# A planned diffusion layer in float32: the first small loads go to ScalarE's queue, single features' weights to another ring, and the planner gets other times for warm-ups and for the probabilities' trip

## The chip, the cores and the metric

The kernel runs on one core of one Trainium2 chip. What counts is the time of one execution on the device, in microseconds, as the median of several runs. TensorE (PE) multiplies matrices, VectorE (DVE) and ScalarE (ACT) work elementwise, GpSimd (POOL) does a little set-up work, and SyncE (SP) issues transfers, which 16 DMA engines carry out.

## What is computed

One layer of a diffusion transformer, on 256 latent tokens and 256 context tokens of width 2048, all in float32:

```python
sh1, sc1, g1, sh2, sc2, g2 = ada_mods(c, w_ada, b_ada)          # silu(c) @ w_ada + b_ada; six vectors of 2048
csh1, csc1, ...            = ada_mods(c_ctx, w_ada, b_ada)
qa, ka, va, qb, kb, vb     = mixer_qkv(x * (1 + sc1) + sh1, w_in, ..., rope)        # w_in: 2048 x 3072
qac, kac, vac, ..          = mixer_qkv(ctx * (1 + csc1) + csh1, w_in, ..., None)
heads = concat(window_sink_attention(qa, ka, va, kac, vac, sink), global_attention(qb, kb, vb, kbc, vbc))
x = layer_norm(ALPHA * x + g1 * (heads @ w_out))
x = layer_norm(ALPHA * x + g2 * swiglu(x * (1 + sc2) + sh2, w_gate, w_up, w_down))   # hidden 5632
```

There are 16 query heads of 128 in four groups (two windowed with a sink, two global), each group with its own key and value head. `w_ada` is 2048 x 12288, `w_out` 2048 x 2048.

## The kernel before, in words

**Arithmetic.** A float32 product runs as three products of rounded parts: every operand is split into `hi` (a cast on ACT) and `lo` (the rest, a subtraction on DVE), and `mm3` (L271 to L273) issues `hi x hi`, `lo x hi` and `hi x lo`, each 128x512 on PE. So each weight tile that is loaded (`raw`) costs ACT a cast (L495, L261) and DVE a subtraction (L498, L262) before PE can use it, and its buffer comes free when both are done.

**First stage.** The features of the model are taken in growing groups (1, 1, 2, 4 and 8 blocks of 128). For each group the columns of `sh1` and `sc1` are computed first: `flow_columns` loads pieces of `w_ada` and multiplies them by `cs`, the silu of the two condition vectors, on PE (L546); the sums are copied by ACT (L571), added up on PE (L576) and given their bias `bcol`. Then x and the context are transposed on PE (L633), modulated on ACT (L639), split, and multiplied by the group's rows of `w_in` (`flow_blocks`), whose sums are kept in SBUF between groups. Before the first product PE runs warm-ups (L1130), multiplications of the identity that keep its clock up; `WARM` of them are steps of the plan with the lowest rank.

**Attention.** Sixteen pairs of heads (`flow_attend`: four for each head group) go the same way: scores on PE (six products for two heads), the row maximum on DVE, the exponentials and their weighting on ACT, a transposition in 32x32 squares on DVE (L921), then the probabilities' trip through memory, which puts the squares in order: a *put* of four transfers from `hx` to the scratch `pd` (L927), and a *get* of one transfer from `pd` to `pT` (L932), both issued by SP; the get waits until the put has landed. Then PE multiplies `pT` by the values (L939), and the results feed the output products with `w_out`. Beside all this DVE sums the gate `g1` from `w_ada` (L381), whose loads SP issues too (L371).

**What sets the order.** All steps up to the first FFN products are given to a planner, `Flow`: a step has an engine, a time in ns, steps that it follows, and buffers that it takes and gives back. `forward` runs them through a list schedule, `backward` ranks them by their latest start, eight times in turn, and the best order is written out: each engine executes its steps strictly in that order. On SP a load counts its transfer time (`dma_ns`: 390 bytes per ns for long rows) as the time of its step, and 2000 ns more until others may use it. A pair (step, early) in `after` lets the next step start `early` ns before the usual time, or later where `early` is negative. In the trip the put counts 1800 ns on SP, the get may start 1500 ns (`SLOW`) after it and counts 1300, and the products with the values may start 2000 + 1500 ns after that. `begin` holds the time at which each engine can start.

**Buffers.** `raw` (4) and `araw` (2) are 8 KB for each partition and hold weights as loaded; `hl` (4) holds pairs of hi and lo; `b4` is a ring of 18 buffers of 4 KB that holds operands, keys, `hx`, `pT` and the like. A buffer of a pool whose name ends in `raw` comes back 1300 ns after its last user in the plan (`AGAIN`).

**Start.** SP issues five small loads first: the two condition vectors (`crow`, L311 and L312), the biases (`brow`, L314), and the first blocks of x and of the context (L608, L613), and then the first pieces of `w_ada` and `w_in` (L473). The single features' weights (groups 0 and 1) come in four loads of 1, 2, 2 and 1 blocks of 512 columns, into `raw` or `araw`.

After the plan comes the FFN (L1344 on), in an order written by hand: gate and up products with u2 (`u2h`, `u2l`), then the down products with `hT`.

Of the kernel before, what the change touches and what calls it, by code (L numbers as in the profile page):

```python
# [22 lines left out]
P = 128  # L23
# [13 lines left out]
G4 = 4  # L37
# [8 lines left out]
T2K = 5  # L46
WARM = 56
SLACK = 2500
AHEAD = 14
# [5 lines left out]
SEED_G = 4  # L55
SLOW = 1500


class Buf:

    def __init__(self, *pools):
        self.pools, self.pool, self.left = pools, None, 0

# [5 lines left out]
class Flow:  # L69
# [26 lines left out]
    def forward(self):  # L96
# [11 lines left out]
        while len(order) < len(self.steps):  # L108
# [3 lines left out]
            for e in self.ENGINES:  # L112
# [4 lines left out]
                for item in sorted(ready[e]):  # L117
# [10 lines left out]
                    for b in s.give:  # L128
                        left[b] -= 1
                        if left[b] == 0:  # L130
                            lag = self.AGAIN if b.pool.endswith("raw") else self.OTHER[e]
                            heapq.heappush(back, (free[e] + lag, b.pool))
# [64 lines left out]
def dit_layer(ctx: ExitStack, tc: tile.TileContext, x, c, cx, c_ctx, w_ada, b_ada, w_in, q_norm_g,  # L197
# [112 lines left out]
    crow = pa.tile([2 * KD, P], F32, tag="crow", name="crow")  # L310
    nc.sync.dma_start(crow[0:KD, :], c.rearrange("o (k p) -> (o k) p", p=P))  # L311
    nc.sync.dma_start(crow[KD : 2 * KD, :], c_ctx.rearrange("(k p) -> k p", p=P))  # L312
    brow = pa.tile([6 * KD, P], F32, tag="brow", name="brow")
    nc.sync.dma_start(brow, b_ada.rearrange("o (n p) -> (o n) p", p=P))  # L314
    cps = wk_bank()
# [109 lines left out]
    def const_tables():  # L425
        nc.gpsimd.tensor_scalar_mul(nsink, sinkb, -1.0)
        for t in range(NT):
            for g, cg, sg in ((gq, cosQ, sinQ), (gk, cosK, sinK)):
# [18 lines left out]
    F = Flow({"raw": RAW_BUFS, "araw": ADA_BUFS, "hl": HL_BUFS, "acc": 4, "wk": 4, "b4": NB4, "t2k": T2K},  # L447
             {"SP": 2100.0, "PE": 3800.0, "ACT": 4300.0, "DVE": 4000.0, "POOL": 4000.0})
    pools = {"raw": wraw, "araw": araw}
    qacc = [[pa.tile([P, NB], F32, tag=f"q{gi}{t}", name="qacc") for t in range(NT)] for gi in range(4)]  # L450
# [17 lines left out]
    def flow_load(w, k0, nk, c0, width, where=("raw", "araw")):  # L468
        room = Buf(*where)

        def fn():
            room.t = pools[room.pool].tile([P, G4 * NB], F32, tag="raw", name="raw")[:, : nk * width]
            nc.sync.dma_start(  # L473
                room.t.rearrange("p (k n) -> p k n", k=nk),
                w[k0 * P : (k0 + nk) * P, c0 : c0 + width].rearrange("(k p) n -> p k n", p=P),
            )
# [124 lines left out]
    def flow_part(k0, n, at, each):  # L601
        ns = KD * n * P // (G4 * NB)
        ats = [at + each * 0.8 * (i + 0.5) / ns for i in range(ns)]
        copy, ready = flow_columns(k0 * P, n, shc[:, k0 : k0 + n, :], scc[:, k0 : k0 + n, :], ats, at + 0.8 * each)
        cx_room = Buf("b4")

        def load_x():
# [9 lines left out]
        ns = dma_ns(n * P * SEQ * 4, n * P * 4)  # L617
        loads = [F.add("SP", max(ns, 500), load_x), F.add("SP", max(ns, 500), load_cx, take=[cx_room])]
        for s in range(2):
# [3 lines left out]
            for j0 in range(0, n, 2):  # L623
# [24 lines left out]
                def rest(rooms=rooms, j0=j0, nj=nj, uf=uf):  # L648
                    nc.vector.tensor_tensor(rooms[1].t[:, j0 : j0 + nj, :], uf.t[:, :nj, :],
                                            rooms[0].t[:, j0 : j0 + nj, :].bitcast(F32), op=ALU.subtract)  # L650

                p = F.add("PE", 205 * nj, flip, [loads[s], copy if k0 else None], [ps], [cx_room] if s else [],
                          at=None if k0 else -1.0)
# [50 lines left out]
    def flow_blocks(g, bs, where=("raw", "araw")):  # L704

        k0, n = GROUPS[g]
        if n == 1:
            for i, (b0, m) in enumerate(((2, 1), (0, 2), (3, 2), (5, 1))):
                F.at = bs[0] + (bs[1] - bs[0]) * i / 4
                piece, = flow_weights(w_in, k0, 1, b0 * NB, m * NB, where)  # L710
                for j in range(m):
                    flow_block(g, b0 + j, [(piece, [j * NB])])
            return
# [149 lines left out]
    def flow_attend(gi, at, each):  # L863
# [5 lines left out]
        for p in range(4):  # L869
# [94 lines left out]
            for i in range(2):  # L964
                g.append(F.add("DVE", 615, lambda i=i, f=squares: f(i), [n[i], *g], [hx] if i == 0 else [], [probs[i]]))
            a = F.add("SP", 1800, put, g, give=[hx])
            g = [(F.add("SP", 1300, get, [(a, -SLOW)], [pT]), -SLOW)]
            v = F.add("PE", 1760, values, g, [o_ps], [pT, *kv_room[w]])
# [172 lines left out]
    for i in range(WARM):  # L1141
        warms.append(F.add("PE", 225, lambda i=i: warm_step(i), [warms[-1]], [wps] if i == 0 else [], [wps], at=1e6))

# [481 lines left out]
```

## Time and profile before

| | |
|---|---|
| runs | 1160.09, 1164.0 and 1165.95 us; median 1164.0 |
| span of the profiled execution | 1167.2 us, 3.2 above the median; what lies around the span is not listed |
| PE busy | 1130.9 us, 97% |
| weight loads of PE (PEld) | 912.2 us, 78% |
| DVE busy | 829.0 us, 71% |
| ACT busy | 546.9 us, 47% |
| moved by DMA | 321.28 MB, mean 275 GB/s |

PE busy counts a matmul until its modelled end, and matmuls overlap, so 100% busy is not yet PE at its peak; the weight loads beside it tell more: in stretches where one product follows on another they take some 0.19 us of each 0.23. A wait is told by the idle time before an instruction, with the engine or transfer that ended it. For SP the time of an instruction is that of issuing, not of moving data; DMA share and GB/s of a stretch tell what the engines moved. The mean of the DMA share can lie a little above 1.

### The profile page before, as it was taken

What the parts mean: (1) busy time and instruction counts of PE and PEld (TensorE: products, weight loads), DVE (VectorE), ACT (ScalarE), POOL (GpSimd) and SP (SyncE); (2) the same over time, 40 slices, a digit from 0 to 9 for tenths busy, and PEclk for the clock granted to TensorE, in tenths of its full rate; (3) what the DMA queues carried; (4) which work ended last, traced back from release to release, by engine and by line L of the source; (5) the groups of instructions that cost most, each with busy time, mean ns of one, the idle gap of its engine ahead of it and who ended that gap; (6) DMA issues with size and microseconds to landing.
All of it is one profiled execution on the core that took longest, in us unless ns stands there. A gap on an engine that the chain in (4) does not pass through costs nothing.

```text
span 1167.2 us, 14247 instructions
## 1 busy us (share of the span) xinstructions
PE 1130.9 (97%) x5347; PEld 912.2 (78%) x5347; DVE 829.0 (71%) x1053; ACT 546.9 (47%) x784; POOL 36.8 (3%) x82
## 2 busy tenths in 40 slices
PE   8999999999988989999999999999999999999995
PEld 8767678777866868888878888888888888888884
DVE  4754479899978978777757666676675778676556
ACT  3332454777755345444454444444444334343341
POOL 1000030111000000000000000000000000000000
PEclk9989999999999999999999999999999999999998
DMA  8999999777999859989967666767767988887641
GB/s 262 378 369 349 391 369 349 256 230 222 312 330 331 301 185 327 350 292 309 325 195 252 222 222 223 245 218 259 250 219 250 326 289 320 315 294 246 212 145 72
DMA packets 186271, 321.28 MB, mean 275 GB/s; under 512 B 8621, under 2 KB 51021, under 8 KB 183896
## 3 DMA queue, kind: packets, MB, share of 16 engines
q1 hardware_dynamic: 186200, 320.36, 79.5%
q8 instruction: 42, 0.69, 0.2%
q14 instruction: 29, 0.23, 0.1%
HBM read 304.07 MB, written 16.25 MB: 274 GB/s over the span
## 4 chain that ended last, share of the span: by engine, by line
PE 78%; DMA 9%; DVE 9%; issue 2%; ACT 1%; SPq 1%; DVEq 0%; ACTq 0%
PE acc L271 24%; PE acc L273 24%; PE acc L272 24%; DMA raw<-in_w_ada_dram 5%; PE wk L546 2%; DVE lo L498 2%; DMA pd<-hx 2%; PE wk L1130 1%; DVE g1b L381 1%; DMA pT<-pd 1%; SPq L927 1%; PE wk L939 1%; DVE hx L921 1%; DMA raw<-in_w_in_dram 1%; DVE adav L381 1%
## 5 line engine op out<-in xcount | busy, mean ns | idle before, releaser
L262 DVE TENSOR_TENSOR lo<-raw,hi 128x1024 fp32r<-128x1024 f32 x258 | 312.6, 1221 | 188.1 <-ACT hi L261 184.7
L261 ACT CAST hi<-raw 128x1024 fp32r<-128x1024 f32 x258 | 271.4, 1055 | 355.0 <-PE acc L273 310.4
L272 PE MATMUL acc<-lo,u2h 128*128 128x512 f32 x704 | 275.2, 391 | 2.3 <-DVE lo L262 2.3
L271 PE MATMUL acc<-hi,u2h 128*128 128x512 f32 x704 | 275.6, 391 | 1.2 <-ACT u2h L1448 1.2
L273 PE MATMUL acc<-hi,u2l 128*128 128x512 f32 x704 | 274.9, 391 | 0.0
L272 PEld LDWEIGHTS acc<-lo,u2h 128*128 128x128 f32 x704 | 132.8, 189 | 30.1 <-DVE lo L262 2.7
L271 PEld LDWEIGHTS acc<-hi,u2h 128*128 128x128 f32 x704 | 132.7, 189 | 28.9 <-ACT u2h L1448 1.4
L273 PEld LDWEIGHTS acc<-hi,u2l 128*128 128x128 f32 x704 | 132.8, 189 | 28.2 <-DVE u2l L1449 0.6
L495 ACT CAST hi<-raw 128x1024 fp32r<-128x1024 f32 (+1 forms) x86 | 87.8, 1032 | 120.7 <-DMA raw<-in_w_in_dram 60.3
L271 PE MATMUL acc<-hi,hTh 128*128 128x512 f32 x344 | 135.5, 394 | 0.0
L273 PE MATMUL acc<-hi,hTl 128*128 128x512 f32 x344 | 133.9, 389 | 0.0
L272 PE MATMUL acc<-lo,hTh 128*128 128x512 f32 x344 | 133.9, 389 | 0.0
L381 DVE SCALAR_TENSOR_TENSOR adav<-raw,cs,adav 128x512 f32<-128x512 f32 (+1 forms) x128 | 121.2, 947 | 14.0 <-DMA raw<-in_w_ada_dram 12.3
L498 DVE TENSOR_TENSOR lo<-raw,hi 128x1024 fp32r<-128x1024 f32 (+1 forms) x86 | 101.7, 1196 | 28.9 <-ACT hi L495 28.9
L271 PE MATMUL acc<-hi,uh 128*128 128x512 f32 x256 | 103.1, 403 | 0.2 <-ACT hi L495 0.2
L272 PE MATMUL acc<-lo,uh 128*128 128x512 f32 x256 | 100.5, 393 | 0.8 <-DVE lo L498 0.8
L273 PE MATMUL acc<-hi,ul 128*128 128x512 f32 x256 | 100.4, 392 | 0.0
L272 PEld LDWEIGHTS acc<-lo,hTh 128*128 128x128 f32 x344 | 64.6, 188 | 14.3 <-issue 1.0
L271 PEld LDWEIGHTS acc<-hi,hTh 128*128 128x128 f32 x344 | 64.6, 188 | 14.1 <-issue 0.7
L273 PEld LDWEIGHTS acc<-hi,hTl 128*128 128x128 f32 x344 | 64.6, 188 | 13.5
L271 PEld LDWEIGHTS acc<-hi,uh 128*128 128x128 f32 x256 | 48.5, 189 | 17.3 <-issue 5.8
L272 PEld LDWEIGHTS acc<-lo,uh 128*128 128x128 f32 x256 | 48.4, 189 | 10.6 <-DVE lo L498 1.2
(205 smaller groups left out, 1155.1 us busy)
## 6 DMA issues: line engine op xcount, KB each, us to landing
raw<-in_w_ada_dram SPq DMA_DIRECT2D x72, 1024.0 KB, 7.4
raw<-in_w_gate_dram SPq DMA_DIRECT2D x44, 1024.0 KB, 5.2
raw<-in_w_up_dram SPq DMA_DIRECT2D x44, 1024.0 KB, 5.5
raw<-in_w_down_dram SPq DMA_DIRECT2D x44, 1024.0 KB, 5.0
raw<-in_w_ada_dram SPq DMA_DIRECT2D x48, 512.0 KB, 5.1
raw<-in_w_in_dram SPq DMA_DIRECT2D x18, 1024.0 KB, 6.8
raw<-in_w_out_dram SPq DMA_DIRECT2D x16, 1024.0 KB, 5.7
pd<-hx SPq DMA_DIRECT2D x64, 128.0 KB, 5.7
```

The lines of the kernel that those rows point to most:

```text
L261: nc.scalar.copy(hi[:, :n], raw[:, s : s + n])
L262: nc.vector.tensor_tensor(lo[:, :n], raw[:, s : s + n], hi[:, :n].bitcast(F32), op=ALU.subtract)
L271: nc.tensor.matmul(ps, lhsT=xh, rhs=w[0], start=first, stop=False, skip_group_check=seeded)
L272: nc.tensor.matmul(ps, lhsT=xh, rhs=w[1], start=False, stop=False, skip_group_check=seeded)
L273: nc.tensor.matmul(ps, lhsT=xl, rhs=w[0], start=False, stop=last, skip_group_check=seeded)
L381: nc.vector.scalar_tensor_tensor(a[:, c : c + piece], raw[:, f : f + piece], cs[:, 4 * (g * (G4 * NB // w) + j) + 2, None], a[:, c : c + p ...
L495: nc.scalar.copy(hl.hi[:, :n], raw.t[:, s : s + n])
L498: nc.vector.tensor_tensor(hl.lo[:, :n], raw.t[:, s : s + n], hl.hi[:, :n].bitcast(F32), op=ALU.subtract)
L546: nc.tensor.matmul(bank.t[32 * j : 32 * j + 32, :width], lhsT=cs[:, 4 * k + 2 - 2 * i : 4 * k + 34 - 2 * i], rhs=raw.t[:, c * width : (c + ...
L921: nc.vector.transpose(hx.t[:, i, :].rearrange("p (r k q) -> p k r q", r=4, k=4), probs[i].t.rearrange("p (k r q) -> p k r q", r=4, k=4))
L927: nc.sync.dma_start(st["hd"][:, :, :, a, :].rearrange("r i h x -> i h r x"), hx.t[32 * a : 32 * a + 32].rearrange("i h (r x) -> i h r x", ...
L939: nc.tensor.matmul(o_ps.t[:, : 2 * P].rearrange("p (g q) -> p g q", q=32), lhsT=v, rhs=pv[:, k], start=k == 0, stop=k == 3)
```

## The change

1. The five small loads go from SP to ACT, ahead of ACT's first instruction; the first block of the context goes to the last 128 columns of `xt` for the time being (`first_cx`; x's own last columns are loaded there much later), and the planner no longer has load steps for the first block. SP's begin in the plan goes from 2100 to 900 ns. Three warm-ups stand ahead of the first transposition.
2. The single features' weights come in three loads of two blocks, and only into `b4`; a buffer counts as loaded (`AGAIN`) by the pools that it may use.
3. The first ten planned warm-ups count 430 ns, not 225.
4. The put counts 2700 ns, the get may start 3000 ns after it, and counts 1300 as before; the values' further wait stays at 1500, now `SLOW2`.

The core of the diff:

```diff
+EARLY_WARM = 3
+COLD = 10
-SLOW = 1500
+SLOW = 3000
+SLOW2 = 1500
+PUT_NS = 2700
+GET_NS = 1300
...
-        self.pools, self.pool, self.left = pools, None, 0
+        self.pools, self.pool, self.left, self.loaded = pools, None, 0, "raw" in pools[0]
...
-                            lag = self.AGAIN if b.pool.endswith("raw") else self.OTHER[e]
+                            lag = self.AGAIN if b.loaded else self.OTHER[e]
...
-    nc.sync.dma_start(crow[0:KD, :], c.rearrange("o (k p) -> (o k) p", p=P))
-    nc.sync.dma_start(crow[KD : 2 * KD, :], c_ctx.rearrange("(k p) -> k p", p=P))
+    nc.scalar.dma_start(crow[0:KD, :], c.rearrange("o (k p) -> (o k) p", p=P))
+    nc.scalar.dma_start(crow[KD : 2 * KD, :], c_ctx.rearrange("(k p) -> k p", p=P))
+    nc.scalar.dma_start(xt[:, :, :P], x[:, :P].rearrange("(t p) d -> p t d", p=P))
+    first_cx = xt[:, :, D - P :]
+    nc.scalar.dma_start(first_cx, cx[:, :P].rearrange("(t p) d -> p t d", p=P))
     brow = pa.tile([6 * KD, P], F32, tag="brow", name="brow")
-    nc.sync.dma_start(brow, b_ada.rearrange("o (n p) -> (o n) p", p=P))
+    nc.scalar.dma_start(brow, b_ada.rearrange("o (n p) -> (o n) p", p=P))
+    early = wk_bank()
+    for _ in range(EARLY_WARM):
+        nc.tensor.matmul(early[:, :P], lhsT=ident, rhs=ident, start=True, stop=True)
...
-             {"SP": 2100.0, "PE": 3800.0, "ACT": 4300.0, "DVE": 4000.0, "POOL": 4000.0})
-    pools = {"raw": wraw, "araw": araw}
+             {"SP": 900.0, "PE": 3800.0, "ACT": 4300.0, "DVE": 4000.0, "POOL": 4000.0})
+    pools = {"raw": wraw, "araw": araw, "b4": pa}
...
-            room.t = pools[room.pool].tile([P, G4 * NB], F32, tag="raw", name="raw")[:, : nk * width]
+            if room.pool == "b4":
+                room.t = b4([P, SUB * NB], F32, "raw4")[:, : nk * width]
+            else:
+                room.t = pools[room.pool].tile([P, G4 * NB], F32, tag="raw", name="raw")[:, : nk * width]
...
-        loads = [F.add("SP", max(ns, 500), load_x), F.add("SP", max(ns, 500), load_cx, take=[cx_room])]
+        loads = [F.add("SP", max(ns, 500), load_x), F.add("SP", max(ns, 500), load_cx, take=[cx_room])] if k0 else [None, None]
...
-            for i, (b0, m) in enumerate(((2, 1), (0, 2), (3, 2), (5, 1))):
-                F.at = bs[0] + (bs[1] - bs[0]) * i / 4
-                piece, = flow_weights(w_in, k0, 1, b0 * NB, m * NB, where)
+            for i, (b0, m) in enumerate(((2, 2), (0, 2), (4, 2))):
+                F.at = bs[0] + (bs[1] - bs[0]) * i / 3
+                piece, = flow_weights(w_in, k0, 1, b0 * NB, m * NB, ("b4",))
...
-            a = F.add("SP", 1800, put, g, give=[hx])
-            g = [(F.add("SP", 1300, get, [(a, -SLOW)], [pT]), -SLOW)]
+            a = F.add("SP", PUT_NS, put, g, give=[hx])
+            g = [(F.add("SP", GET_NS, get, [(a, -SLOW)], [pT]), -SLOW2)]
...
-        warms.append(F.add("PE", 225, lambda i=i: warm_step(i), [warms[-1]], [wps] if i == 0 else [], [wps], at=1e6))
+        warms.append(F.add("PE", 430 if i < COLD else 225, lambda i=i: warm_step(i), [warms[-1]], [wps] if i == 0 else [], [wps], at=1e6))
```

Since the planner works with other times, the order of every engine changes up to the FFN. Two places on SP matter most.

The first is the start of SP's program. In the kernel before, the rows up to the second pair of `w_ada` pieces are these (128x16x128 is a piece of 1 MB of one block's columns):

```order
L311 DMA crow<-in_c_dram 16x128
L312 DMA crow<-in_c_ctx_dram 16x128
L314 DMA brow<-in_b_ada_dram 96x128
L608 DMA xt<-in_x_dram 128x2x128
L613 DMA cxt<-in_ctx_dram 128x2x128
L473 DMA raw<-in_w_ada_dram 128x16x128 x2
L473 DMA raw<-in_w_in_dram 128x512
L473 DMA raw<-in_w_in_dram 128x1024 x2
```

In the changed kernel SP's program starts so (L487 is the same line as L473 before; raw_185, raw_190 and raw_211 lie in `b4`; 128x8x256 is a piece for a group of two blocks):

```order
L487 DMA raw<-in_w_ada_dram 128x16x128 x2
L487 DMA raw_185<-in_w_in_dram 128x1024
L487 DMA raw_190<-in_w_in_dram 128x1024
L487 DMA raw_211<-in_w_in_dram 128x1024
L487 DMA raw<-in_w_ada_dram 128x16x128 x2
L487 DMA raw<-in_w_ada_dram 128x8x256 x2
```

The five small loads have left the head of the queue, and two more pairs of `w_ada` pieces stand right behind the first weights. On ACT the five loads stand ahead of the table load and of everything else, in this order: the two condition vectors, x, the context, the biases. On PE 21 warm-ups stand ahead of the first products with `w_ada` before and 9 after, and 46 and 40 ahead of the first product with `w_in`.

The second place is the probabilities' trips, as SP has them from the fourth put on, in the kernel before (pd<-hx are the four transfers of a put, pT<-pd is a get, and the numbers tell which get belongs to which put):

```order
L927 DMA pd_2352<-hx_2306 64x4x128 x4
L932 DMA pT_2396<-pd_2352 128x1024
L473 DMA raw_2454<-in_w_out_dram 128x4x512
L927 DMA pd_2479<-hx_2458 64x4x128 x4
L932 DMA pT_2527<-pd_2479 128x1024
L473 DMA raw_2545<-in_w_out_dram 128x4x512
L927 DMA pd_2590<-hx_2540 64x4x128 x4
L932 DMA pT_2639<-pd_2590 128x1024
```

And in the changed kernel, from the fourth put on (L942 is the put, L947 the get, L382 a load for the gate):

```order
L942 DMA pd_2259<-hx_2215 64x4x128 x4
L947 DMA pT_2301<-pd_2171 128x1024
L382 DMA raw_2309<-in_w_ada_dram 128x2048
L947 DMA pT_2345<-pd_2259 128x1024
L487 DMA raw_2359<-in_w_out_dram 128x4x512
L942 DMA pd_2419<-hx_2398 64x4x128 x4
L487 DMA raw_2461<-in_w_out_dram 128x4x512
L947 DMA pT_2508<-pd_2419 128x1024
L942 DMA pd_2535<-hx_2499 64x4x128 x4
L487 DMA raw_2580<-in_w_out_dram 128x4x512
L947 DMA pT_2633<-pd_2535 128x1024
```

Before, each get stands right behind its own put; now a load or another pair's transfer stands between. Over the whole attention that is so: 6 of the 16 gets stood right behind their puts before and 1 after, and between put and get of the 11th, 12th, 13th and 16th pair there now stand 2 to 2.5 MB of other transfers, where 1 MB stood before. PE's order was moved with it: between the last score product of a pair and its first product with the values there stand on average 78.8 products of 128x512 before (60 to 108) and 94.9 after (60 to 132); the mean of the first eight pairs goes from 81.0 to 99.8, that of the last eight from 76.5 to 90.0, and three pairs lose (the fifth and the fifteenth 12 each, the tenth 6).

More of the change, by code (lines that the diff above doesn't have):

```diff
@@ L605, in flow_part @@
         cx_room = Buf("b4")
+        cx_room.t = first_cx
         def load_x():
@@ L650, in rest @@
                                             rooms[0].t[:, j0 : j0 + nj, :].bitcast(F32), op=ALU.subtract)
-                p = F.add("PE", 205 * nj, flip, [loads[s], copy if k0 else None], [ps], [cx_room] if s else [],
+                p = F.add("PE", 205 * nj, flip, [loads[s], copy if k0 else None], [ps], [cx_room] if s and k0 else [],
                           at=None if k0 else -1.0)
```

## The prediction

> **What bounds the kernel now.** I read the page first, then the busy time by stages, then the chain of waits and SP's rows for the two places that the change touches. The page says that PE is what the span is made of, and that the DMA engines are nearly full through the first third:
>
> ```profile
> span 1167.2 us, 14247 instructions
> ...
> PE 1130.9 (97%) x5347; PEld 912.2 (78%) x5347; DVE 829.0 (71%) x1053; ACT 546.9 (47%) x784; POOL 36.8 (3%) x82
> ...
> DMA  8999999777999859989967666767767988887641
> ```
>
> By stages (stretch, its length, busy time and instructions of PE, weight loads, DVE, ACT and POOL, granted clock, DMA share, GB/s):
>
> ```profile
> 0.00:20.00 20.00, 16.87 (x166) 16.05 (x167) 5.73 (x9) 6.14 (x12) 3.48 (x9) 1.00 0.74 224
> 20.00:150.00 130.00, 127.39 (x773) 88.61 (x772) 70.99 (x102) 44.91 (x69) 0.00 (x0) 0.97 1.01 372
> 150.00:240.00 90.00, 90.00 (x421) 73.56 (x422) 80.98 (x114) 57.52 (x108) 15.69 (x28) 1.00 0.86 316
> 240.00:300.00 60.00, 56.60 (x265) 45.08 (x265) 55.35 (x114) 42.69 (x112) 7.99 (x26) 1.00 0.74 225
> 300.00:400.00 100.00, 91.69 (x397) 73.46 (x396) 83.11 (x110) 56.61 (x93) 0.56 (x3) 0.98 1.00 340
> 400.00:480.00 80.00, 76.33 (x360) 60.55 (x359) 64.26 (x94) 38.89 (x58) 3.19 (x6) 0.98 0.75 262
> 480.00:1100.00 620.00, 617.69 (x2736) 510.25 (x2735) 429.65 (x460) 279.12 (x309) 5.85 (x10) 1.00 0.77 264
> ```
>
> Five stages with three limits. From 20 to 150 the DMA share is 1.01: the weights' arrival sets the pace, and PE's weight loads fill only 68% of the time against 82% afterwards. From 150 to 240 PE has no idle time. In the attention, 240 to 400, PE is idle for 160 - 56.60 - 91.69 = 11.7 us, with DMA slack in the first 60 us (share 0.74) and none in the last 100 (1.00). From 480 on PE is full and the change touches nothing. So whatever the first 400 us win or lose reaches the end whole.
>
> **The start.** The chain of waits runs through PE's warm-ups (start, length, what; two records each):
>
> ```profile
> 3.83 1.76 PE wk L1130 x8
> ...
> 6.88 4.61 PE wk L1130 x32
> ...
> 12.49 2.65 PE wk L1130 x22
> ...
> 17.14 2.56 PE wk L1130 x22
> 19.70 0.23 PE acc L271
> ```
>
> A warm-up takes 1.76 / 4 = 0.44 us at first and 2.65 / 11 = 0.24 later, where the plan has 225 ns: by the plan PE was free sooner than it was. But from 20 us on DMA is the limit, so what counts in the start is when the transfers begin and whether they go on. SP's rows (start, length of issuing):
>
> ```profile
> 0.74 0.39 SPq L311 DMA_DIRECT2D crow<-in_c_dram  x1
> ...
> 3.09 0.47 SPq L473 DMA_DIRECT2D raw<-in_w_ada_dram  x1
> 3.60 1.65 SPq L473 DMA_DIRECT2D raw<-in_w_ada_dram  x1
> 5.29 3.65 SPq L473 DMA_DIRECT2D raw<-in_w_in_dram  x1
> ...
> 15.76 0.43 SPq L473 DMA_DIRECT2D raw<-in_w_ada_dram  x1
> ```
>
> The first large load is issued at 3.09, behind five small ones; and the next pair of `w_ada` pieces at 15.76, when a buffer is free. Between, the DMA engines run dry (same columns as above):
>
> ```profile
> 13.00:14.00 1.00, 1.00 (x12) 1.00 (x11) 0.00 (x0) 0.45 (x1) 0.00 (x0) 1.00 0.54 209
> 14.00:15.00 1.00, 1.00 (x11) 0.95 (x9) 0.69 (x1) 0.16 (x1) 0.00 (x0) 1.00 0.03 12
> 15.00:16.00 1.00, 1.00 (x34) 0.81 (x32) 0.00 (x0) 0.00 (x0) 0.00 (x0) 1.00 0.25 16
> 16.00:17.00 1.00, 1.00 (x17) 0.92 (x9) 0.00 (x0) 0.78 (x2) 0.00 (x0) 1.00 0.66 127
> ```
>
> *Term 1.* The changed SP starts with the large loads: 3.09 - 0.74 = 2.35 us. With the single features' weights in `b4` the six 8 KB buffers are left to `w_ada`, and 4 MB of it and 1.5 MB of `w_in` can be issued before any buffer must come back: 15 us at the 372 GB/s of the next stage, which reaches over the hole: 0.46 + 0.97 + 0.75 + 0.34 = 2.5 us. The small loads still have to be moved, beside the large ones now:
>
> ```profile
> xt<-in_x_dram SPq DMA_DIRECT2D x2, 128.0 KB
> cxt<-in_ctx_dram SPq DMA_DIRECT2D x2, 128.0 KB, 2.5
> brow<-in_b_ada_dram SPq DMA_DIRECT2D x1, 48.0 KB, 1.7
> ```
>
> One of each is 304 KB, 0.8 us at 372 GB/s. So 2.35 + 2.5 - 0.8 = 4.0 us of lead. Two later holes can go or grow with the new order:
>
> ```profile
> 85.00:90.00 5.00, 5.00 (x22) 4.22 (x21) 3.37 (x5) 4.06 (x9) 0.00 (x0) 0.76 0.56 172
> 100.00:105.00 5.00, 5.00 (x39) 1.90 (x38) 2.75 (x4) 0.00 (x0) 0.00 (x0) 1.00 0.74 251
> ```
>
> They lose 5 x 0.44 + 5 x 0.26 = 3.5 us. Bounds of the term: 0, if ACT's queue is slow (a rival below); 7.5, if these two holes close as well, which nothing says. The Trainium skill (DMA: Bandwidth & Descriptors, § Issuing engines are not separate DMA queues) says that DMAs of several issuers share the same engines, so that a second issuer saves only issuing time. By that alone the term would be 2.35; the hole is closed by buffers, which the page doesn't speak of.
>
> The rest of the start is free. What follows ACT's issues now, and when the first columns are multiplied:
>
> ```profile
> 1.05 1.28 ACT L319 ACT_TABLE_LOAD   x1 [1.05 <-DVE cs L318]
> 3.20 0.23 ACT L319 ACTIVATE cs<-wk 128x32 f32<-128x32 f32 x1 [0.87 <-PE wk L316]
> ...
> 11.41 1.08 PE L546 MATMUL wk<-raw,cs 128*32 128x128 f32 x32
> ```
>
> Five issues of 0.4 us each (as the first of SP's rows) from 0.74 on, the table load and the silu end at 0.74 + 2.0 + 1.28 + 0.23 = 4.3 us, long before 11.41. Three early warm-ups end before the condition arrives. Fewer warm-ups stand before the first products; if PE is idle there, it waits for DMA, and DMA is the limit. The `b4` ring gives five buffers while nearly nothing else is in it. One cast and one subtraction fewer in each of the two groups lie on engines that are half idle up to 150 us (DVE 70.99 of 130). If the ring were full after all, the loads would wait for it as they waited for `raw`, and the hole's 2.5 us would stay.
>
> **The attention.** Who waits for the trip, from 240 to 400 (a group: busy, mean ns, idle before it and what ended it; a wait: us in total, times, longest):
>
> ```profile
> L939 PE MATMUL wk<-pT,kvacc 128*128 128x256 f32 x128 | 32.4, 398 | 10.1 <-DMA pT<-pd 8.5 <-ACT pr L901 1.6
> ...
> PE wk L939 <- DMA pT<-pd: 8.5, 5, 3.0
> ...
> SPq L932 <- DMA pd<-hx: 54.3, 26, 4.9
> ```
>
> 10.1 of the 11.7 us are waits for the probabilities, none over 3.0. And SP stands for 54.3 us before gets, with other loads behind it, while the DMA share is 0.74. One trip in full:
>
> ```profile
> 281.50 2.57 SPq L927 DMA_DIRECT2D pd<-hx  x4
> 286.66 0.33 SPq L932 DMA_DIRECT2D pT<-pd  x1
> ...
> pT<-pd SPq DMA_DIRECT2D x16, 512.0 KB, 4.0
> ```
>
> 2.57 of issuing, 2.6 of landing, 0.33, 4.0 of landing: 9.5 us, and more where four transfers land in up to 4.9 us: 11.8. The old plan had 1800 + 1500 + 1300 + 3500 = 8.1, the new one has 10.5. It still falls short of the longer trips, but by about 1 us and not 4.
>
> *Term 2.* In PE's order a pair has 94.9 products between its scores and its values instead of 78.8; at 0.23 us each (the last row of the chain above) that is 3.7 us more room on average, above the longest wait of 3.0. Where gets no longer stand right behind their puts, loads fill SP's standing time. Against that, two pairs lose 12 products, 2.8 us each, and in the stage with a full DMA share a later get lands later. I take back all of the 3.4 us that PE is idle from 240 to 300, where DMA has room, and a quarter of the 8.3 from 300 to 400, where it has none: 5.5 us. Bounds: 11.7 at best; a loss of 8 at worst (last rival).
>
> *Term 3.* From 400 to 480 PE is idle for 3.7 us around the layer norm. The order of the loads there changes a little; I put 0, within 2 either way.
>
> **Sum.** 4.0 + 5.5 + 0 = 9.5 us off the profiled span of 1167.2, which gives 1157.7. The span lies 3.2 above the median of 1164.0; the same 9.5 off the median gives **1154.5**. A change under 0.5%, 5.8 us, can hardly be told from none here: the runs of before lie 5.9 apart.
>
> **Rivals.** *DMA holds the attention* (20%). From 300 to 400 its share is 1.00, and the bytes before the last put are nearly the same as before. If PE's waits only move to the weights of the output products, term 2 is 0 and the result 1160. For it: the full share. Against it: SP's 54.3 us.
>
> *ACT's loads are stuck behind SP's* (13%). Issuing took 1.65 and 3.65 us in the rows above when the large pieces had filled the queue, against 0.4 otherwise. If each of ACT's five issues lets one of SP's large ones pass, ACT is free after some 10 us of SP's issuing and 2 of its own. The silu would come at about 14 us and the first columns 3 later than the 11.41 of now; the buffers come back that much later, and term 1 shrinks from 4.0 to about 1: 1157.5. The Trainium skill (Perfetto Trace Analysis, § DMA Instruction — HWDGE (DVE, Sync)) has such a rule: the block that generates descriptors is shared by the two issuers and locked by one instruction at a time. SP's long issues agree with it, but no row here has two issuers.
>
> *The trip becomes too long* (7%): slower. The place is 300 to 400, where four of the last pairs (11th, 12th, 13th, 16th) now have 2 to 2.5 MB between put and get instead of 1. At 340 GB/s 1 MB more takes 3.1 us, the same as the 13.5 products of more room that the last eight pairs have. From the point where the loads ahead of a get take longer than that room, PE waits each time. If those four pairs wait the 3.1 us more each and nothing else is won, 12.4 us come on top, less the 4.0 of the start: 1172.
>
> **How the numbers follow.** My forecast, both terms in good part, has 60%, with a range of its own from 1147 to 1159. The cases besides: 1160 (20%), 1157.5 (13%), 1172 (7%). Faster by over 0.5% means under 1158.2: nearly all of the first case (0.57), half of the third (0.07) and a little of the second (0.04), 0.68 together. Slower by over 0.5% means above 1169.8: 0.05. Same: 0.27. The range goes from 1147, where both terms reach near their better bounds, to 1163, which takes in the first two rivals; the last one (7%) and the ends, among them both bounds at once, are left out.
>
> **What would show it.** Right: the first large load issued before 1 us, no slice of 1 us with a DMA share under 0.8 from 6 to 20 us, the first product with `w_in` 2 to 4 us before the 19.70 of now, the stage up to 150 us shorter by 4; PE's idle time before the values under 5 us and SP's before gets well under 54.3. Wrong: the silu after 10 us (second rival); PE's idle time moved from the values to the output products or the casts (first rival); waits for the trip over 3 us from 300 on (third rival).

## The result, and the profile after

The changed kernel takes 1145.5 us (median of four runs, 1145.02 to 1147.06) against 1165.0 for the kernel before (1160.09 to 1168.19): 19.4 us less, ratio 0.9838, 95% interval 0.9812 to 0.9864. That is about twice the 9.5 us of the forecast and 1.5 below its range. Of the profiled executions the one after spans 1145.3 us, 21.9 less. From its page:

```profile
span 1145.3 us, 14227 instructions
...
PE 1120.7 (98%) x5353; PEld 906.2 (79%) x5353; DVE 828.6 (72%) x1051; ACT 546.6 (48%) x782; POOL 37.5 (3%) x82
...
DMA  9899999596999879989967667677687988877531
```

The span less PE's busy time is PE's idle time: 24.6 us after, 1167.2 - 1130.9 = 36.3 before, so 11.7 of the 21.9 us. The view of the cores (span, mean granted clock) has most of the rest, first before and then after:

```profile
core 0: 1167.2 us, clock 0.989
```

```profile
core 0: 1145.3 us, clock 0.996
```

By these means, 1167.2 x 0.011 - 1145.3 x 0.004 = 8.3 us less were lost to a lower clock of PE, an estimate. The prediction had no such term. By stages after (columns as in the prediction):

```profile
0.00:20.00 20.00, 11.96 (x127) 10.93 (x128) 4.89 (x7) 5.49 (x9) 3.48 (x9) 1.00 0.96 297
20.00:150.00 130.00, 129.94 (x831) 92.66 (x829) 73.71 (x103) 47.05 (x72) 0.00 (x0) 1.00 0.98 366
150.00:240.00 90.00, 90.00 (x421) 73.39 (x421) 81.85 (x122) 58.78 (x113) 17.02 (x28) 1.00 0.83 306
240.00:300.00 60.00, 60.00 (x285) 49.01 (x284) 57.92 (x113) 43.25 (x109) 6.79 (x26) 1.00 0.82 270
300.00:400.00 100.00, 97.55 (x447) 76.37 (x446) 89.99 (x128) 56.73 (x95) 1.08 (x4) 1.00 0.95 338
400.00:480.00 80.00, 79.67 (x364) 65.77 (x365) 66.56 (x81) 44.03 (x62) 3.34 (x5) 1.00 0.86 307
480.00:1100.00 620.00, 619.24 (x2749) 511.70 (x2748) 424.84 (x456) 278.94 (x308) 5.84 (x10) 1.00 0.77 262
```

The start got worse for PE (8.0 us idle in the first 20, 3.1 before) and better for DMA (297 GB/s, 224 before). The attention is full: 2.5 us idle instead of 11.7. What became of the waits there (the group from 240 to 400, then SP's wait over the whole execution, as the 54.3 before is):

```profile
L954 PE MATMUL wk<-pT,kvacc 128*128 128x256 f32 x128 | 30.1, 380 | 0.8 <-DVE oTl L965 0.8
```

```profile
SPq L947 <- DMA pd<-hx: 15.0, 20, 2.4
```

No wait for the trip is left, and SP stands 15.0 us before gets instead of 54.3. Why PE starts later, in the timeline after (start, length, what):

```profile
0.73 2.32 SPq L487 DMA_DIRECT2D raw<-in_w_ada_dram  x2
...
0.73 0.45 ACTq L316 DMA_DIRECT2D crow<-in_c_dram  x1
...
2.88 0.49 ACTq L322 DMA_DIRECT2D brow<-in_b_ada_dram  x1
...
6.70 0.23 ACT L330 ACTIVATE cs<-wk 128x32 f32<-128x32 f32 x1 [1.95 <-PE wk L327]
...
9.97 0.42 PE L345 MATMUL wk<-ident,brow 96*128 96x96 f32 x1 [3.31 <-DMA brow<-in_b_ada_dram]
...
22.77 0.48 PE L276 MATMUL acc<-hi,uh 128*128 128x512 f32 x1
...
24.91 10.48 SPq L487 DMA_DIRECT2D raw<-in_w_ada_dram  x2
```

SP's large loads go out at 0.73, as forecast, and ACT issues its five in half a microsecond each. But they land late. The condition of the context took 5.0 us, so the silu comes at 6.70 (3.20 before). The biases, issued at 2.88, are there only at 9.9, seven microseconds later (1.7 before); their transposition stands in PE's order ahead of that of x, of six warm-ups and of the first columns, which start at 13.39 (11.41 before), and the first product with `w_in` comes at 22.77 (19.46 before). The two rows before:

```profile
3.41 0.42 PE L334 MATMUL wk<-ident,brow 96*128 96x96 f32 x1 [0.25 <-DMA brow<-in_b_ada_dram]
...
19.46 0.48 PE L271 MATMUL acc<-hi,uh 128*128 128x512 f32 x1
```

Buffers come back later too, SP stands at 24.91 for 10.48 us, and DMA runs dry:

```profile
32.00:34.00 2.00, 2.00 (x13) 1.41 (x15) 0.71 (x2) 1.23 (x3) 0.00 (x0) 1.00 0.13 38
34.00:36.00 2.00, 2.00 (x72) 1.91 (x73) 1.81 (x2) 0.94 (x2) 0.00 (x0) 1.00 0.00 0
```

The biggest surprise lies where the forecast looked for nothing. In the kernel before, at the entry to the FFN and at 610 us:

```profile
417.94 0.75 DVE L381 SCALAR_TENSOR_TENSOR adav<-raw,cs,adav 128x512 f32<-128x512 f32 x1
...
421.33 0.55 DVE L1065 TENSOR_SCALAR xt<-xt,mv,ly 128x512 f32<-128x512 f32 x1
...
422.02 1.08 PE L1300 MATMUL wk<-ident,xt 128*128 128x128 f32 x4 [2.49 <-DVE xt L1065]
...
607.74 0.69 DVE L1344 SCALAR_TENSOR_TENSOR xt<-xt,lgb 128x512 f32<-128x512 f32 x1 [3.60 <-DMA lgb<-in_ln_g_dram]
...
612.09 4.62 DVE L262 TENSOR_TENSOR lo<-raw,hi 128x1024 fp32r<-128x1024 f32 x4
...
613.36 0.80 PE L272 MATMUL acc<-lo,u2h 128*128 128x512 f32 x1 [2.31 <-DVE lo L262]
```

DVE worked on other things while PE stood: four sums of the late modulation (L381) between the steps of the layer norm, and near 610 the residual of the second layer norm (L1344), for whose vector DVE stood 3.60 us itself, with the low halves of the FFN's weights behind it. And each wait has a tail: PE's clock is lower for a while after it. In two-microsecond windows of the kernel before, from the end of the first wait on (granted clock third from the right):

```profile
422.02:424.02 2.00, 2.00 (x7) 1.80 (x8) 0.00 (x0) 1.27 (x4) 0.00 (x0) 0.50 0.83 207
424.02:426.02 2.00, 2.00 (x11) 1.66 (x10) 0.00 (x0) 1.55 (x4) 0.00 (x0) 0.67 0.92 355
```

That is 2 x 0.50 + 2 x 0.33 = 1.7 us more, so a wait of 2.49 us costs 4.1. In the kernel after the same two places read:

```profile
PE acc L277 <- DVE lo L267: 0.8, 1, 0.8
PE wk L1315 <- DVE xt L1080: 0.3, 1, 0.3
```

No clock drop follows them. Neither place is in the diff. Up to the first FFN products the planner's order is kept; what is written behind it is ordered by the framework's scheduler, which may also set DVE work between the planned steps. So the order there is not simply that of the source, as the section on the kernel before has it, and it moved with the plan.

### The profile page after: what moved, and what is told of

Same layout as the page of the kernel before. It is cut to its first block, busy times and chain, and to the rows that moved or that the text cites. A ratio compares the mean times of both kernels' runs of the same rounds, so it can differ in the third digit from the quotient of the medians.

```text
span 1145.3 us, 14227 instructions
## 1 busy us (share of the span) xinstructions
PE 1120.7 (98%) x5353; PEld 906.2 (79%) x5353; DVE 828.6 (72%) x1051; ACT 546.6 (48%) x782; POOL 37.5 (3%) x82
## 4 chain that ended last, share of the span: by engine, by line
PE 90%; DVE 4%; DMA 3%; issue 1%; ACT 1%; SPq 0%; ACTq 0%; DVEq 0%
PE acc L276 27%; PE acc L277 27%; PE acc L278 27%; PE wk L560 3%; DMA raw<-in_w_ada_dram 2%; PE wk L1145 1%; PE wk L954 1%; DVE adav L392 1%; PE wk L648 1%; DMA brow<-in_b_ada_dram 1%; DMA lgb<-in_ln_b_dram 1%; DVE lo L512 1%; PE wk L276 0%; PE wk L278 0%; PE wk L1007 0%
## 5 line engine op out<-in xcount | busy, mean ns | idle before, releaser
L267 DVE TENSOR_TENSOR lo<-raw,hi 128x1024 fp32r<-128x1024 f32 x258 | 312.4, 1220 | 182.8 <-ACT hi L266 179.4
L266 ACT CAST hi<-raw 128x1024 fp32r<-128x1024 f32 x258 | 271.3, 1055 | 351.2 <-PE acc L278 307.3
L509 ACT CAST hi<-raw 128x1024 fp32r<-128x1024 f32 x84 | 87.1, 1050 | 106.2 <-PE acc L278 58.4
L512 DVE TENSOR_TENSOR lo<-raw,hi 128x1024 fp32r<-128x1024 f32 x84 | 101.1, 1218 | 22.2 <-ACT hi L509 21.9
L277 PE MATMUL acc<-lo,uh 128*128 128x512 f32 x256 | 99.8, 390 | 0.0
L278 PEld LDWEIGHTS acc<-hi,ul 128*128 128x128 f32 x256 | 48.1, 188 | 10.3
```

Of the source, the lines that this page charges most:

```text
L266: nc.scalar.copy(hi[:, :n], raw[:, s : s + n])
L267: nc.vector.tensor_tensor(lo[:, :n], raw[:, s : s + n], hi[:, :n].bitcast(F32), op=ALU.subtract)
L277: nc.tensor.matmul(ps, lhsT=xh, rhs=w[1], start=False, stop=False, skip_group_check=seeded)
L278: nc.tensor.matmul(ps, lhsT=xl, rhs=w[0], start=False, stop=last, skip_group_check=seeded)
L509: nc.scalar.copy(hl.hi[:, :n], raw.t[:, s : s + n])
L512: nc.vector.tensor_tensor(hl.lo[:, :n], raw.t[:, s : s + n], hl.hi[:, :n].bitcast(F32), op=ALU.subtract)
```

## The experiments

Each ratio is to the kernel before, run on the same chip, with its 95% interval.

**The parts alone.** The first run is the kernel before with the trip's new times only:

```diff
-SLOW = 1500
+SLOW = 3000
+SLOW2 = 1500
+PUT_NS = 2700
+GET_NS = 1300
...
```

> The kernel before with part 4 of the change alone (put 2700, get 3000 later). In its order the room of a pair grows to 99.2 products on average (78.8 before, 94.9 with the whole change) and no get stands right behind its put. Theory A (the trip's planned times carry the gain in the attention): 1150 us within 3 beside 1165 before; PE idle before the values from 240 to 400 us under 3 us, SP's waits before gets under 25 us; the first 240 us as before within 0.5. Theory B (the whole order changed with the start, and the attention won by the other data that the planner got): 1160 to 1165, with PE's idle time there still over 8 us.

Measured: 1145.1 us, 0.985 (0.9825 to 0.9875): all of the change's gain, from this part alone. SP stands 11.2 us before gets, PE waits for no trip. Both of my expectations were too high, and the first 240 us did not stay as they were: measured as in the table under "Why the prediction was wrong", the start ends 2.9 us later than the mean of the kernel before, the attention is 15.0 shorter, and the two places in the FFN are 7.8 shorter. The second run is the rest of the change:

```diff
-SLOW = 3000
+SLOW = 1500
-PUT_NS = 2700
+PUT_NS = 1800
```

> The changed kernel with part 4 undone (put 1800, get 1500 later): small loads on ScalarE, weights in the 4 KB ring, cold warm-ups. Room of a pair 81.0 products, 4 of 16 gets right behind their puts. Theory A: 2 us off by the start and little in the attention, 1160 to 1164; PE idle before the values 7 to 12 us. Theory B: 1147 to 1152, with the attention as short as in the changed kernel.

Measured: 1153.4 us, 0.9922 (0.9907 to 0.9937), between the two theories. With -17 and -9 us the parts add up to more than the whole, so some gain is in both. The same two FFN waits are short or gone in both runs.

**The order of DVE in the FFN.** The kernel before, with DVE held to the written order from the end of the planned region (the framework's manual region, for DVE alone) to the end of the late sums:

```diff
     region.__exit__(None, None, None)
+    dve_order = tc.manual_schedule(engines={ET.DVE})
+    dve_order.__enter__()
...
     run(merge(first_half[3 : 2 * ONE_F], scales))
+    dve_order.__exit__(None, None, None)
```

> The kernel before, with DVE held to the written order at the entry to the FFN, so that the four late modulation sums (L381, 0.74 us each) come behind the second half of the layer norm instead of between its steps; further on the scheduler then also puts only three residual steps in a row ahead of the low halves near 610 us, where before has six. Theory (the loss at the entry and at 610 is a matter of DVE's order): PE's wait for the normalised rows falls from 2.5 us to under 0.5, first FFN product to the 48th takes 13 us instead of 17.0, the 704th to the 840th 35 instead of 38.5; the time falls by 3.8 + 3.0 = 6.8 us, ratio 0.994. Rival (the sums hold buffers, so that putting them back only delays the loads behind them): PE waits as long a little later, ratio 1.000.

Measured: 1158.0 us, 0.994 (0.9916 to 0.9964), as the theory said; its waits in the FFN:

```profile
PE acc L272 <- DVE lo L262: 0.8, 1, 0.8
PE wk L1300 <- DVE xt L1065: 0.3, 1, 0.3
```

In the other run the region ends only ahead of the FFN's main loop:

```diff
+    dve_order.__exit__(None, None, None)
     flips = []
```

> As the run beside it, but DVE is held to the written order up to the FFN's main loop. The sums stand behind the layer norm here too, but near 610 us six residual steps still stand ahead of the low halves. Theory: the entry's 3.8 us are won, of the 3.0 at 610 nothing or a part: 1.0 to 3.8 less than the run beside it, ratio 0.9965. Rival (the place is not what costs the time at 610, or holding DVE to its written order costs more than it brings): as the run beside it, or slower than before.

Measured: 1176.4 us, 1.0114 (1.0087 to 1.014): slower, which only the rival allowed for. The entry is mended here as well (0.3 us of waiting), but the place at 610 got worse and a third one appeared:

```profile
605.18 0.69 DVE L1344 SCALAR_TENSOR_TENSOR xt<-xt,lgb 128x512 f32<-128x512 f32 x1 [3.88 <-DMA lgb<-in_ln_g_dram]
...
609.47 0.80 PE L272 MATMUL acc<-lo,u2h 128*128 128x512 f32 x1 [7.77 <-DVE lo L262]
...
451.63 0.80 PE L272 MATMUL acc<-lo,u2h 128*128 128x512 f32 x1 [6.05 <-DVE lo L262]
```

So the order on DVE sets this loss, and holding it can win or lose. The two waits of the kernel before are not chance: profiled twice more, unchanged,

> The kernel before, unchanged, profiled a second time. Theory (the losses at the entry to the FFN and at 610 us come from DVE's order, the clock drop at 80 us was chance): PE waits again 2.5 us for the normalised rows and 2.2 to 2.3 for the low halves, each with some 4 us of lower clock behind it; at 80 us the clock stays at 1.00 and the 600th product with w_in starts at 201 to 203 us instead of 205.7. Rival (all of these are chance of one execution): other waits at other places.

> The same once more, with the same expectations: 2.5 and 2.2 to 2.3 us of waiting in the FFN again, clock 1.00 at 80 us.

it took 1167.6 and 1163.0 us and waited 2.5 us for the normalised rows both times, and 2.0 and 2.2 us for the low halves. Chance was a wait at 80 us: the first profile has 1.68 us there with a clock of 0.62, 0.50, 0.50 and 0.68 in the 8 us behind it, which is 3.4 us; the first new one has 1.71 us there with the clock at 1.00, the second 0.43 us of waiting.

**The start, part by part.** The ring alone (the weights of groups 0 and 1 into `b4`, in three loads, on the kernel before, with the pool's code as in the change), and the small loads on ACT alone (the kernel after with ring, warm-up times and trip set back):

```diff
...
-            for i, (b0, m) in enumerate(((2, 1), (0, 2), (3, 2), (5, 1))):
+            for i, (b0, m) in enumerate(((2, 2), (0, 2), (4, 2))):
...
-                piece, = flow_weights(w_in, k0, 1, b0 * NB, m * NB, where)
+                piece, = flow_weights(w_in, k0, 1, b0 * NB, m * NB, ("b4",))
```

> The kernel before with one part of the change alone: the single features' weights go to the 4 KB ring, in three loads instead of four. Small loads stay on SP, trip and warm-ups as before. Theory (the start is set by buffers, the small loads' landing costs what ACT's issuing saves): the DMA hole of 2.5 us between 13 and 17 us closes and the start gains 2 to 3 us; the FFN's order is planned anew and its 6.8 us go as in the other variants: -9 us, ratio 0.992; with the old order in the FFN -2.5, ratio 0.998. Rival (the two early large loads of ACT's part are what gives the start its gain): the start gains nothing.

```diff
-COLD = 10
+COLD = 0
-SLOW = 3000
+SLOW = 1500
-PUT_NS = 2700
+PUT_NS = 1800
...
-            for i, (b0, m) in enumerate(((2, 2), (0, 2), (4, 2))):
+            for i, (b0, m) in enumerate(((2, 1), (0, 2), (3, 2), (5, 1))):
...
-                piece, = flow_weights(w_in, k0, 1, b0 * NB, m * NB, ("b4",))
+                piece, = flow_weights(w_in, k0, 1, b0 * NB, m * NB, where)
```

> The kernel after with the ring, the planned warm-up times and the trip's times undone: what is left is that ACT issues the first small loads and SP begins with the large ones. Theory: the bias rows land at 7 to 9 us beside the large loads instead of 4, PE waits 3 us for them, the hole between 13 and 17 us stays or grows; the start wins 0 (between -1.5 and +1.5) against before. With the FFN planned anew 1158, ratio 0.994; with the old order there 1165, ratio 1.000. Rival (the early large loads carry the start's gain): the start gains 2.35 us or more.

Measured: 1166.6 us, 1.0005 (0.9988 to 1.0021), and 1157.4, 0.9942 (0.9928 to 0.9957). In the ring's run the FFN keeps both waits of the kernel before (2.5 and 2.2 us), in ACT's run it has neither. In ACT's run the two places in the FFN are 9.8 us shorter and the 701st product of all comes 2.9 later than the mean of the kernel before, so its 6.7 us are those of the FFN. In the ring's run the hole at 13 to 17 us is closed (no 1-us slice from 12 to 19 is under 0.98), and the 701st product comes 1.1 earlier, less than three profiles of the kernel before lie apart (3.9). So neither part wins anything at the start that can be told. Then the kernel after with the condition and the biases back on SP, ahead of the large loads, the planned order unchanged:

```diff
-    nc.scalar.dma_start(crow[0:KD, :], c.rearrange("o (k p) -> (o k) p", p=P))
-    nc.scalar.dma_start(crow[KD : 2 * KD, :], c_ctx.rearrange("(k p) -> k p", p=P))
+    nc.sync.dma_start(crow[0:KD, :], c.rearrange("o (k p) -> (o k) p", p=P))
+    nc.sync.dma_start(crow[KD : 2 * KD, :], c_ctx.rearrange("(k p) -> k p", p=P))
...
-    nc.scalar.dma_start(brow, b_ada.rearrange("o (n p) -> (o n) p", p=P))
+    nc.sync.dma_start(brow, b_ada.rearrange("o (n p) -> (o n) p", p=P))
```

> The changed kernel, but the condition vectors and the biases (three of the five small loads) are issued by SP again, ahead of its large loads; x and the context stay on ScalarE. The planned order is the same to the last row. Theory A (a small load that shares the engines with large ones lands late, holds PE's queue, and the buffers that come back late make the hole in the DMA share at 32 to 36 us): biases land 3 us after the start and not 10, the first product with w_in 3 to 4 us earlier than the 22.8 us of the changed kernel, the hole at 32 to 36 us gone, large loads 1.4 us later: in all 2 to 3 us faster than the changed kernel, 1142 to 1144. Rival (the first 150 us are set by the DMA engines' bytes alone and the hole has another cause): 1.4 us slower than the changed kernel, 1147.

Measured: 1142.8 us, 0.9841 (0.982 to 0.9863); that could not be told from the kernel after on another chip, so both ran once more, side by side and oftener:

> The kernel after, with the condition and the bias rows issued by SP ahead of the large loads, in more rounds beside the kernel after itself. Theory (PE's late start costs the end about as much as the trace shows): 3 to 6 us less than the kernel after, ratio to before 0.980. Rival (the lead of 4 us at the first product is given back at the next place where data bounds it): the same as the kernel after, within 1.5 us.

> The kernel after, unchanged, as the yardstick for the three runs beside it. Every theory: the ratio of before, 0.984, within 0.003.

Measured: 1143.6 us, 0.9825 (0.9798 to 0.9851), and 1146.7, 0.9851 (0.9821 to 0.988): 3.1 us less than the kernel after, 21.9 less than before, the fastest version here. Its timeline and the two windows that were empty:

```profile
4.25 0.42 PE L345 MATMUL wk<-ident,brow 96*128 96x96 f32 x1 [0.51 <-DMA brow<-in_b_ada_dram]
...
18.50 0.47 PE L276 MATMUL acc<-hi,uh 128*128 128x512 f32 x1
```

```profile
32.00:34.00 2.00, 2.00 (x31) 1.32 (x24) 1.33 (x3) 0.82 (x1) 0.00 (x0) 1.00 1.05 359
34.00:36.00 2.00, 2.00 (x20) 2.00 (x20) 0.64 (x4) 1.62 (x4) 0.00 (x0) 1.00 1.09 400
```

The biases are there at 4.2 instead of 9.9, the first product starts 4.3 us earlier and the hole is gone. So the late small loads cost 3.1 us, most of what the start was forecast to win.

**The trip: PE's room or SP's standing?** The kernel after with other times (in ns; SLOW is how much later a get starts in the plan, SLOW2 the same for the values). Each run changes one to three of these lines, as the table's second column has them; the last two, for instance:

```diff
-SLOW2 = 1500
+SLOW2 = 0
-GET_NS = 1300
+GET_NS = 400
```

```diff
-SLOW = 3000
+SLOW = 1500
-PUT_NS = 2700
-GET_NS = 1300
+PUT_NS = 1800
+GET_NS = 2800
```

> The changed kernel with the get allowed 4500 ns after the put and not 3000. Room of a pair 102.0 products, no get right behind its put, up to 3 MB between them. Theory A: the waits are gone already at 3000, so nothing more is to be won: 1145.5 within 3, PE idle before the values under 3 us. Rival (each us of planned trip still buys time): 1142 or less. Second rival (loads between put and get now delay the values): over 1149, with waits for the trip again.

> The kernel after with the overlap set back (SLOW 1500 instead of 3000); the longer put (2700) stays. 87.6 products stand between scores and values on average instead of 94.9 (81.0 with both set back), but hardly a get stands right behind its put. Theory A (what counts is the room on PE): the 7.9 us between both set back (1153.4) and the kernel after (1145.5) over 13.9 products are 0.57 us a product, so 3.8 of 7.9 are won: 1149.6, ratio 0.988. Theory B (what counts is that SP no longer stands before gets): nearly all is won, 1146.5, ratio 0.985, with SP's wait before gets near the 15 us of the kernel after.

> The kernel after with the put's time set back (1800 instead of 2700); the longer overlap (3000) stays. 85.7 products of room on average, three pieces of get right behind a put. Theory A (room on PE): 2.7 of 7.9 us are won, 1150.7, ratio 0.989. Theory B (SP's standing): little is won, 1152.5, ratio 0.9915, with SP's wait before gets near the 40 us of the run with both set back.

> The kernel after with times for the trip that keep gets away from their puts without giving PE room: put 2700 and overlap 3000 as after, but the get's own time 400 instead of 1300 and its values planned without the 1500 of SLOW2. 78.9 products between scores and values on average (81.0 with the trip's times set back, 94.9 after), two pieces of get right behind a put, 1.4 MB between put and get on average. Theory A (room on PE): nothing is won against the run with both set back, ratio 0.992; PE waits 5 us or more for the probabilities, though SP stands only about 20 us before gets. Theory B (SP's standing): as after, ratio 0.986, PE waits under 1 us.

> The kernel after with the trip's put and overlap set back (1800, 1500) and the get's time raised from 1300 to 2800: the same total of 10.6 us for the trip as the kernel after, put in at another of its steps. 102.0 products of room on average. Theory A (room on PE): as after or a little better, ratio 0.985, PE waits for the probabilities under 1 us, whatever SP does. Theory B (SP's standing): SP stands some 30 to 40 us before gets, since the put's time is the old one, and the time stays near 0.991.

| run | put, get, SLOW, SLOW2 | products between scores and values | SP before gets, us | values wait for the trip, us | median, us | ratio (interval) |
|---|---|---|---|---|---|---|
| start_only | 1800, 1300, 1500, 1500 | 81.0 | 40.0 | 5.2 | 1153.4 | 0.9922 (0.9907 to 0.9937) |
| no_room | 2700, 400, 3000, 0 | 78.9 | 23.3 | 2.2 | 1153.2 | 0.9919 (0.9892 to 0.9946) |
| slow_only | 1800, 1300, 3000, 1500 | 85.7 | 21.4 | 0.9 | 1147.6 | 0.9854 (0.9825 to 0.9883) |
| put_only | 2700, 1300, 1500, 1500 | 87.6 | 19.8 | 0.4 | 1148.3 | 0.987 (0.9841 to 0.9899) |
| after_again | 2700, 1300, 3000, 1500 | 94.9 | 15.0 | 0 | 1146.7 | 0.9851 (0.9821 to 0.988) |
| get_2800 | 1800, 2800, 1500, 1500 | 102.0 | 28.5 | 0 | 1148.1 | 0.9872 (0.9848 to 0.9896) |
| slow_4500 | 2700, 1300, 4500, 1500 | 102.0 | 6.4 | 0 | 1146.6 | 0.9863 (0.9849 to 0.9878) |

(The waits of `after_again` are those of the first profile after.) `slow_only` and `put_only` could not tell the theories apart, since each shortened SP's standing and gave room, and both won nearly everything; my price per product was wrong. `no_room` and `get_2800` do. Without room, SP's standing fell as low as with `slow_only` and nothing was won; with room, 28.5 us of standing cost nothing that these runs can tell. Their groups, `no_room` first:

```profile
L954 PE MATMUL wk<-pT,kvacc 128*128 128x256 f32 x128 | 31.5, 390 | 4.3 <-DMA pT<-pd 2.2 <-ACT acc L524 1.9 <-ACT pr L916 0.3
```

```profile
L954 PE MATMUL wk<-pT,kvacc 128*128 128x256 f32 x128 | 30.4, 380 | 0.2 <-ACT pr L916 0.2
```

The loss lies in the attention: from the 701st product to the last output product it took 172.2 us in `start_only` and 171.9 in `no_room`, against 166.5 in `slow_only` and 164.8 in `get_2800`. One part of the expectation for `no_room` missed: PE waits only 2.2 us for the trip and not 5 or more. It waits for ACT besides, 1.9 us for a copy of sums (L524) and 1.8 for the cast of a pair's result (L961); in `get_2800` neither wait is left. So PE's room decides, for a pair's whole chain and not for the trip alone. From about 86 products on more of it brings nothing that these runs can tell.

## Why the prediction was wrong

To set off one execution's chance, here are three profiles of the kernel before and two of the kernel after (starts in us of single products of 128x512 in PE's rows: the 701st of all, the last output product, and the 49th, 705th and 841st of the FFN's gate and up):

| | 701st | last output | FFN 49th | 705th | 841st |
|---|---|---|---|---|---|
| before | 231.3 | 409.4 | 432.1 | 584.4 | 622.9 |
| before_look1 | 228.6 | 406.8 | 430.9 | 583.2 | 621.5 |
| before_look2 | 227.5 | 403.4 | 426.1 | 578.4 | 616.9 |
| after | 229.2 | 393.8 | 413.1 | 565.4 | 600.9 |
| after_again | 228.3 | 392.7 | 412.1 | 564.4 | 600.0 |

Differences of the means: start 0.4 us, attention 177.4 - 164.5 = 12.9, entry to the FFN 23.2 - 19.4 = 3.8, from there to the 705th product nothing, the stretch around 610 38.4 - 35.5 = 2.9. The sum is 20.0, the medians differ by 19.4.

- **Term 1, the start, forecast 4.0: about 0.** Its parts happened, the early loads and the closed hole at 13 to 17 us (no 1-us slice from 6 to 20 is under 0.94), but the first product with `w_in` came 3.3 us later and not 2 to 4 earlier. The step that failed is the 0.8 us for moving the small loads and "The rest of the start is free": it priced their bytes and their issuing, not when they land beside 1 MB loads, and not who stands behind them on PE. With the condition and the biases first, the 701st product came at 226.8 (`cond_again`) and 224.5 (`cond_sp`), 2.3 and 4.6 before the mean of the kernel before, so the lead itself was there to be had. That the hole's 2.5 us are worth as much is not shown: in the ring's run, with the hole closed, the 701st product came only 1.1 earlier, within the spread of the kernel before. Why is open. The two later holes, at 85 and at 100 us, read as the kernel's, belonged to that one execution: in the two other profiles of it the share of these stretches is 0.98 to 1.05.
- **The second rival** named the place and the silu's lateness, but another cause. The Trainium skill (Perfetto Trace Analysis, § DMA Instruction — HWDGE (DVE, Sync)) has the descriptor block locked by one instruction at a time; by that ACT would be held up while SP's long issues last. SP's second issue ran from 1.23 to 3.05 us, and ACT's third and fourth lay within it, at 0.45 and 0.50 us each, so the trace does not show that here. The landing was late, not the issuing.
- **Term 2, the attention, forecast 5.5: 12.9.** The mechanism is the forecast one, room on PE above the longest wait, and `no_room` and `get_2800` show it, though some of the waits that went with it are for ACT and not for the trip. The failed step is the discount: "a quarter of the 8.3 from 300 to 400, where it has none" took a DMA share of 1.00 for a limit on PE. More bytes went out from 240 to 300 (270 GB/s instead of 225), and from 300 on the share is still 0.95 with PE waiting for no transfer: the share was full, and did not hold PE. So the first rival (DMA holds the attention) fell with the discount that was made for it. And the waits were priced at their own length, without the lower clock behind some of them; that is how the gain can exceed the 11.7 us named as the best (the profile before has one such fall in the attention, worth 1.7 us).
- **Term 3 and "From 480 on PE is full and the change touches nothing": 3.8 + 2.9 instead of 0.** This was the other half of the miss. The profile before showed the waits (PE's 3.7 us of idle time from 400 to 480 and 2.3 from 480 on), but they were read as given, because the diff does not name that code. `ln_first`, which changes only DVE's order, shows the cause: it won 6.1 us of them.
- **The third rival** (trip too long) did not come: `slow_4500`, with still more between put and get, took 1146.6 us and has no wait for the trip.
- Which edit moves the FFN's order is not settled further than the runs go: the trip's times do, ACT's part does, the ring does not. Why the scheduler answers so was not tried, and the warm-ups' planned times (part 3) were not run alone.

## What to carry to other kernels

A change to a planner's times is also a new draw for everything that is ordered behind it: compare the order and the waits of the stages that the diff does not name before attributing the time, and look there for waits of 2 us and more that are only a matter of order. A wait is removed by work put between, on the engine that waits; a full transfer queue is no reason to discount that, unless the trace shows that engine waiting for those transfers. Small loads on which everything else starts belong ahead of the large ones; here that was worth 3.1 us.

## What the hardware showed

- A wait of PE costs more than its length if the clock falls after it. Worked out from windows of 2 us, such a fall cost 1.6 to 1.7 us, as 3.4 us at half the clock would; two of them cost 3.3 and 3.4, twice that. In the three profiles of the kernel before and that of `ln_first`, from 24 to 660 us, the clock fell after 13 of the 22 waits from 1.68 to 3.07 us, among them every one at the entry to the FFN and at 610 in the kernel before. It did not fall after the nine others, up to 3.06 us long, and never after a wait under 1.6. The Trainium skill (TensorE: Matmul & The Clock Gate, § HAM oscillation — how this bites in real kernels) puts the limit at idle gaps of some 3.4 us; all of these were shorter, so there the measurement decides. That the clock has only two steps, half and full, and is set in windows of some 3.4 us (the Trainium skill, TensorE: Matmul & The Clock Gate, § What's actually happening), agrees with the price of 1.7.
- A load of 48 KB took 1.7 us to land with nothing large before it, and about 7 when issued on ACT's queue at 2.88 us, 2 us behind SP's first loads of 1 MB; 8 KB took up to 5.0:

```profile
crow<-in_c_dram ACTq DMA_DIRECT2D x1, 8.0 KB, 3.6
crow<-in_c_ctx_dram ACTq DMA_DIRECT2D x1, 8.0 KB, 5.0
```

  In `cond_again` two loads of 128 KB, issued on ACT's queue at 0.73 and 1.21 us, ahead of SP's first large load at 2.10, took 2.4 us each. So ACT's queue alone is not what made the others late.

- The same program differs from one execution to the next, in part by such clock drops: the three profiles of before span 1167.2, 1165.8 and 1161.2 us at a mean granted clock of 0.989, 0.989 and 0.992. The two of after, whose clock stays at 1.00 from 24 to 1100 us, span 1145.3 and 1144.4.
